# A one-core encoder layer in split fp32: a new order around the norms, the attention fills and the last norm

## The chip, the cores and the metric

The kernel runs on one core of a Trainium2 chip, in one launch. The metric is the device time of one execution in microseconds, as the median of several executions. The core has engines that run side by side, each through a fixed list of instructions: TensorE (PE, matrix products), VectorE (DVE), ScalarE (ACT) and GpSimd (POOL). SyncE (SP) issues most of the DMA transfers; a few are issued from ACT's list. An instruction that waits for a semaphore holds up all that stands behind it on its engine.

## The reference, cut to what matters

x is 512 x 1024 in float32, the inner width of each feed-forward part (FFN) is 2816. The attention projects the normed x to eight heads of differential attention (group A: two score maps for each head, with a relative bias) and eight query heads on two key/value heads (group B: normed and rotated q and k). Every matrix product is wanted at nearly float32 accuracy.

```
def rms_norm(x, g):
    xf = x.astype(jnp.float32)
    y = xf * lax.rsqrt(jnp.mean(xf * xf, axis=-1, keepdims=True) + EPS)
    return (y * g.astype(jnp.float32)).astype(x.dtype)
...
x = x + 0.5 * swiglu(rms_norm(x, ffn1_norm[l]), ffn1_w_gate[l], ffn1_w_up[l], ffn1_w_down[l])
h = rms_norm(x, mix_norm[l])
proj = h @ w_in[l]
...
x = x + jnp.concatenate([oa, ob], axis=-1) @ w_out[l]
x = x + 0.5 * swiglu(rms_norm(x, ffn2_norm[l]), ffn2_w_gate[l], ffn2_w_up[l], ffn2_w_down[l])
return rms_norm(x, final_norm)
```

## The kernel before

**Products.** Every float32 operand is split into two fp32r parts, hi and lo: ACT casts hi (L101), DVE subtracts to get lo (L102), both in `Blocks.parts`. `mm3` (L217) then makes one product of three matmuls. Weights come in blocks: `Blocks.load` (L93, from SP) brings a raw block, two raw buffers deep, and `convert` splits it; `get` hands a block over and, unless `further=False`, splits the next one and loads one more ahead.

**FFN.** x lives in four tiles xn[0..3] of 128 x 1024. The FFN's gate and up products run by a Strassen-like scheme on quarters A11, A12, A21, A22 of the normed, transposed x and on sums S1 to S4 of them (`one_block`); each quarter and sum has hi and lo. The first of the eleven blocks (`first_blocks`) is computed plainly so that it can start while the sums are made. `down` (adds at L484) finishes the tiles in the order t = 2, 3, 0, 1, each in two column halves.

**Norms.** `root` squares a tile on ACT (L292) with a row sum, adds and scales on DVE (L271, L273), and POOL raises to the power -1/2 (L274). `half_T` multiplies (z, L301) and PE transposes z into PSUM (xt, L304). There the gain is per partition, a column `gcol` (L260, an element-wise load, three of them on SP), so `gained` evicts 128 x 256 pieces with ACT (hi, L311) and DVE (lo, L312). `left_first` does tiles 0 and 1 (A11, A12), `left_second` tiles 2 and 3 (A21, A22, S1: L341, L342), `left_sums` the other sums with their splits (L351 to L354). `mix_half` is the same for the attention's input xm.

**Attention.** 64 units (32 of A, then 32 of B; one head and 128 queries each) are written out by hand in a loop, and PE takes that order. Unit i's scores (L743 to L758, L820 to L823), the join of its weights (L768 to L776, L828), the transpose of its weights three units later, its product with v four or five later, and between them fill work by an amount of `FILLS` for each group of units: the remaining projections in `FILL_ORDER`, then the first part of the output projection. The A heads need q and k stacked by DMA (`stack`, L625, 12 issues for each s and head, four for each tile pair); the B heads need k transposed (`make_k2`, PE hT_k, after the 16th step of qb0) and q transposed and copied by DMA (`B_heads`, hT_q and L808, three units ahead). The A output of a pair is normed (o, L794 to L798) and transposed (ot, `finish_O`) seven units behind (`LAG_O`).

**After it.** `out_proj(1)` needs the last B pair (otB); its tiles po_4 to po_7 are added to xn at L916, and after the second of them `half_done` starts FFN2's `left_first`. After the last `down`, `finish` norms each tile for the output: squares, DVE xg = xn * G (L1034), DVE low half (L1038), ACT high half (L1040), issues at L1041.

The order of all engines outside the hand-written loop is set by a planner that goes by priorities and a model of durations; `issue_after` forbids it to place something ahead of a given instruction, `keep_in_program_order` fixes it.

Of the kernel before, what the change touches and what calls it, by code (L numbers as in the profile page):

```python
# [11 lines left out]
F32 = mybir.dt.float32  # L12
# [17 lines left out]
FILL_ORDER = ("qk1", "qk2", "va1", "qk3", "kv", "qb0", "qb1")  # L30
# [4 lines left out]
FILLS = (3.0, 3.0, 3.0, 2.6, 1.3, 1.1, 1.1, 1.1, 2.0)  # L35
LAG_T = 3
LAG_V = {"A": 4, "B": 5}
LAG_O = 7
# [34 lines left out]
class Blocks:  # L73
# [49 lines left out]
    def gate_up(self, t, shape, name):  # L123
# [12 lines left out]
        self.parts(hi[:, 0:4, :], lo[:, 0:4, :], t[:, 0:4, :])  # L136
        for p, n in ((7, 3), (6, 2), (4, 4)):
# [18 lines left out]
def build(ctx, tc, a, out):  # L156
# [92 lines left out]
    def gain_rows(src):  # L249
        g = fpool.tile([P, D], F32, tag="ut", name="G", bufs=1)  # L250
        nc.sync.dma_start(out=g, in_=src.partition_broadcast(P))
# [5 lines left out]
    gcol = {}  # L257
    for nm in ("ffn1", "mix", "ffn2"):
        gcol[nm] = const.tile([P, NK], F32, name=f"gcol_{nm}")
        nc.sync.dma_start(out=gcol[nm], in_=a[f"{nm}_norm"][0].rearrange("(k p) -> p k", p=P))  # L260
        if nm == "ffn1":
            for t in (2, 3):
                nc.sync.dma_start(out=xn[t], in_=xv[:, t, :])
            blocks.load(2)
# [30 lines left out]
    def half_T(half, tags, tag, between=None, parts=2):  # L295

        ps = [bank(tags[kp], f"xt_{tag}{half}{kp}") for kp in range(4)]
        for i in range(2):
            t = 2 * half + i
            r, z = root(t, tag, parts)  # L300
            nc.vector.tensor_scalar_mul(z, xn[t], r)  # L301
            for k in range(NK):
                c = 256 * (k % 2) + P * i
# [14 lines left out]
    def left_first(g, tag, between=None, parts=2):  # L318

        ps = half_T(0, "DDBB", tag, between, parts)  # L320
# [4 lines left out]
        for k in range(NK):  # L325
            gained(L["A11" if k < 4 else "A12"], k % 4, ps[k], g[:, k:k + 1])
        for k in range(NK):
            nc.scalar.activation(raw["A11" if k < 4 else "A12"][:, k % 4, :], ps[k], AF.Copy, scale=g[:, k:k + 1])
        return L, raw

    def left_second(L, raw, g, tag, parts):

        ps = half_T(1, "BCDD", tag, None, parts)
# [42 lines left out]
    def first_blocks(i, L, raw, Hj, g1, second):  # L376
# [23 lines left out]
        for m in "gu":  # L400
            products(m, 1)
# [657 lines left out]
```

## Time and profile before

| | |
|---|---|
| median of 3 executions | 1015.74 us (1014.93 to 1016.44) |
| the profiled execution | 1015.6 us, of which the span is 1013.8 us |
| mean granted TensorE clock | 0.988 |
| busy PE / DVE / ACT / POOL | 974.1 / 720.6 / 489.0 / 227.9 us |
| FFN1 | 0 to 366 us |
| mix norm, first projections | 366 to 407 us |
| attention, A units and B units | 407 to 545 and 545 to 632 us |
| rest of the output projection, FFN2 | 632 to 1003.7 us |
| last norm and output behind the last matmul | 1003.7 to 1013.8 us |

The span runs from the first to the last recorded instruction of the core; the execution's own time has 1.8 us around it. A row of the timeline gives start, duration, engine, line, operation, output<-inputs, and in brackets how long the engine sat idle before it and which instruction ended that wait.

### The profile page before, as it was taken

What the parts mean: (1) busy time and instruction counts of PE and PEld (TensorE: products, weight loads), DVE (VectorE), ACT (ScalarE), POOL (GpSimd) and SP (SyncE); (2) the same over time, 40 slices, a digit from 0 to 9 for tenths busy, and PEclk for the clock granted to TensorE, in tenths of its full rate; (3) what the DMA queues carried; (4) which work ended last, traced back from release to release, by engine and by line L of the source; (5) the groups of instructions that cost most, each with busy time, mean ns of one, the idle gap of its engine ahead of it and who ended that gap; (6) DMA issues with size and microseconds to landing.
All of it is one profiled execution on the core that took longest, in us unless ns stands there. A gap on an engine that the chain in (4) does not pass through costs nothing.

```text
span 1013.8 us, 16666 instructions
## 1 busy us (share of the span) xinstructions
PE 974.1 (96%) x6540; PEld 893.7 (88%) x6540; DVE 720.6 (71%) x1156; ACT 489.0 (48%) x845; POOL 227.9 (22%) x222
## 2 busy tenths in 40 slices
PE   7999999999999999999899989899999999999995
PEld 7999999999888888799888777699999999988884
DVE  5998899988232173777988886689999887842224
ACT  7555444445231162776766665574444454622213
POOL 1232223220000000122656442033222323000001
PEclk8999999999999999999999999999999999999998
DMA  8145534323223325545412121114433423233212
GB/s 244 52 127 188 179 108 126 116 93 109 99 83 106 102 79 144 139 116 158 136 54 58 27 63 52 43 42 125 126 103 106 126 83 125 84 111 118 83 42 83
DMA packets 82399, 105.45 MB, mean 104 GB/s; under 512 B 7873, under 2 KB 66753, under 8 KB 82321
## 3 DMA queue, kind: packets, MB, share of 16 engines
q1 hardware_dynamic: 81744, 103.35, 33.1%
q8 instruction: 51, 0.84, 0.4%
q10 hardware_dynamic: 576, 1.05, 0.3%
q14 instruction: 28, 0.22, 0.1%
HBM read 93.86 MB, written 6.32 MB: 99 GB/s over the span
## 4 chain that ended last, share of the span: by engine, by line
PE 83%; DVE 6%; issue 3%; ACT 2%; DMA 2%; POOL 2%; SPq 1%; POOLq 0%; DVEq 0%; ACTq 0%
PE dn L217 23%; PE bg L217 6%; PE cu L217 6%; PE dg L217 6%; PE du L217 6%; PE bu L217 6%; PE cg L217 6%; PE po L217 3%; PE pqk L217 3%; PE au L217 3%; PE ag L217 3%; PE pva L217 2%; PE poA L217 2%; PE poB L217 1%; PE g L217 1%
## 5 line engine op out<-in xcount | busy, mean ns | idle before, releaser
L102 DVE TENSOR_TENSOR lo_d<-raw_d,hi_d 128x1024 fp32r<-128x1024 f32 x44 | 52.2, 1219 | 84.9 <-ACT hi_d L101 84.9
L132 POOL TENSOR_TENSOR T_g<-raw_g 128x512 f32<-128x512 f32 x40 | 69.1, 1727 | 156.8 <-DVE tl_u L102 75.7
L101 ACT CAST hi_d<-raw_d 128x1024 fp32r<-128x1024 f32 x44 | 44.1, 1051 | 89.8 <-PE dn L217 87.3
L132 POOL TENSOR_TENSOR T_u<-raw_u 128x512 f32<-128x512 f32 x40 | 55.0, 1374 | 128.4 <-DVE tl_g L102 88.9
L101 ACT CAST th_u<-T_u 128x512 fp32r<-128x512 f32 x60 | 37.2, 620 | 88.8 <-PE bg L217 44.6
L101 ACT CAST th_g<-T_g 128x512 fp32r<-128x512 f32 x60 | 37.0, 620 | 46.6 <-PE cu L217 26.5
L758 ACT ACTIVATE s_A<-s_A,m_A 128x512 f32<-128x512 f32 x64 | 45.9, 721 | 25.3 <-DVE m_A L756 25.2
L102 DVE TENSOR_TENSOR lo_g<-raw_g,hi_g 128x1024 fp32r<-128x1024 f32 x44 | 55.7, 1272 | 1.0 <-ACT hi_g L101 0.9
L101 ACT CAST hi_g<-raw_g 128x1024 fp32r<-128x1024 f32 x44 | 44.7, 1047 | 23.6 <-PE dg L217 11.4
L102 DVE TENSOR_TENSOR tl_u<-T_u,th_u 128x512 fp32r<-128x512 f32 x60 | 54.7, 912 | 0.0
L102 DVE TENSOR_TENSOR lo_u<-raw_u,hi_u 128x1024 fp32r<-128x1024 f32 x44 | 53.2, 1216 | 1.6 <-ACT hi_u L101 1.4
L102 DVE TENSOR_TENSOR tl_g<-T_g,th_g 128x512 fp32r<-128x512 f32 x60 | 52.6, 879 | 0.0
L101 ACT CAST hi_u<-raw_u 128x1024 fp32r<-128x1024 f32 x44 | 44.3, 1052 | 15.0 <-PE du L217 12.1
L756 DVE CUSTOM_DVE_ANT_0 s_A<-sA,T 128x512 f32<-128x512 f32 x64 | 42.0, 684 | 9.5 <-PE sA L217 7.5
L829 POOL TENSOR_TENSOR p_B<-p_B,m_B 128x512 f32<-128x512 f32 x32 | 34.5, 1083 | 38.3 <-DVE m_B L828 30.9
L217 PE MATMUL pqk<-xm,hi_qk 128*128 128x512 f32 x128 | 40.3, 396 | 0.0
L217 PEld LDWEIGHTS poA<-va,PT_A 128*128 128x128 f32 x256 | 32.4, 195 | 3.7 <-ACT PT_A L720 3.1
L274 POOL TENSOR_TENSOR r_fin<-r_fin,mhalf 128x1 f32<-128x1 f32 x4 | 2.5, 638 | 145.4 <-DVE r_fin L273 145.4
L217 PE MATMUL poA<-va,PT_A 128*128 128x64 f32 x256 | 33.0, 273 | 2.2 <-ACT PT_A L720 2.2
L274 POOL TENSOR_TENSOR r_mx<-r_mx,mhalf 128x1 f32<-128x1 f32 x4 | 2.2, 552 | 145.0 <-DVE r_mx L273 145.0
L439 ACT ACTIVATE g<-g 128x1024 f32<-128x1024 f32 x20 | 21.2, 1061 | 18.3 <-DVE g L437 18.2
L217 PE MATMUL pqb<-hi_qb,xm 128*128 128x256 f32 x128 | 29.3, 298 | 0.0
(667 smaller groups left out, 3765.3 us busy)
## 6 DMA issues: line engine op xcount, KB each, us to landing
raw_d<-ffn_w_down SPq DMA_DIRECT2D x22, 1024.0 KB, 4.9
raw_g<-ffn_w_gate SPq DMA_DIRECT2D x21, 1024.0 KB, 5.5
raw_u<-ffn_w_up SPq DMA_DIRECT2D x21, 1024.0 KB, 5.4
toep<-nbd SPq DMA_DIRECT2D x8, 512.0 KB, 8.5
raw_qk<-w_in SPq DMA_DIRECT2D x8, 512.0 KB, 4.7
raw_o<-w_out SPq DMA_DIRECT2D x4, 1024.0 KB, 5.5
T<-toep SPq DMA_DIRECT2D x8, 448.0 KB, 4.1
xn<-x SPq DMA_DIRECT2D x4, 512.0 KB, 4.6
```

Of the source, the lines that this page charges most:

```text
L101: self.nc.scalar.copy(out=hi, in_=src)
L102: self.nc.vector.tensor_sub(lo, src, hi.bitcast(F32))
L132: eng.tensor_sub(b12 if n == 1 else T[n], x, T[2] if n == 4 else y)
L217: i = nc.tensor.matmul(*args, **kw)
L274: last["pool"] = nc.gpsimd.tensor_tensor(out=r, in0=r, in1=mhalf[:, 0:1], op=ALU.pow).ins
L439: nc.scalar.activation(g1, g1, AF.Silu)
L756: nc.vector.tensor_tensor_reduce(out=sc, in0=ps, in1=T[:, 384 - P * qt:896 - P * qt], scale=1.0, scalar=BIG, op0=ALU.add, op1=ALU.min, acc ...
L758: nc.scalar.activation(sc, sc, AF.Exp, bias=m[:, s:s + 1], scale=-1.0, accum_out=l1[:, qt, h:h + 1] if s == 0 else l2)
L829: nc.gpsimd.tensor_mul(u["P"], u["P"], l.to_broadcast([P, S]))
```

## The change

- **FFN1's norm.** One gain column is left, loaded from ACT's list ahead of everything; the two others are gone. The transposes of tiles 2 and 3 are held behind the evictions of tiles 0 and 1, the first weight split behind z, and the splits of the sums S behind the main weight split.
- **Mix norm and FFN2's norm.** The gain is loaded as rows (G, 128 x 1024, 512 KB) and multiplied into z by one two-input DVE instruction before the transposes; eviction then takes plain pieces of 128 x 512 (L324, L331), half as many.
- **Attention.** kv's projection is moved ahead of va1 and qk3, make_k2 to the 8th step of qb0, FILLS are given for each four units, the A outputs are transposed nine units behind instead of seven, the B heads are made five units ahead instead of three (three for the first).
- **FFN2's start.** The last block of w_out is got without splitting further; `half_done` runs one tile later; FFN2's first weight split follows z.
- **Last norm.** A fixed order: squares by ACT, low half by DVE straight from xn (L1113), high half of tiles 0 and 1 by DVE and ACT, of tiles 2 and 3 by ACT and a POOL multiplication by G (L1122).

```diff
-FILL_ORDER = ("qk1", "qk2", "va1", "qk3", "kv", "qb0", "qb1")
+FILL_ORDER = ("qk1", "qk2", "kv", "va1", "qk3", "qb0", "qb1")
-FILLS = (3.0, 3.0, 3.0, 2.6, 1.3, 1.1, 1.1, 1.1, 2.0)
+FILLS = (3.0, 3.0, 3.0, 3.0, 3.0, 3.0, 3.0, 2.2, 1.0) + 7 * (1.2,) + (1.4, 1.4)
-LAG_O = 7
+LAG_O = 9
+LEAD_B = (3, 5, 5, 5, 5, 5, 5, 5)
...
-    def gain_rows(src):
...
+    def rows_of(pool, nm, **kw):
+
+        g = pool.tile([P, D], F32, name=f"G_{nm}", **kw)
+        nc.sync.dma_start(out=g, in_=a[f"{nm}_norm"][0].partition_broadcast(P))
         return g
 
+    gcol = const.tile([P, NK], F32, name="gcol")
+    nc.scalar.dma_start(out=gcol, in_=a["ffn1_norm"][0].rearrange("(k p) -> p k", p=P))
     nc.sync.dma_start(out=xn[0], in_=xv[:, 0, :])
...
-            nc.vector.tensor_scalar_mul(z, xn[t], r)
+            if G is None:
+                i = nc.vector.tensor_scalar_mul(z, xn[t], r)
+            else:
+                i = nc.vector.scalar_tensor_tensor(out=z, in0=xn[t], scalar=r, in1=G, op0=ALU.mult, op1=ALU.mult)
+            last["z"] = i.ins
...
+    def evict(hi, lo, p, kp, G):
+
+        for e, col in pieces(kp, G):
+            last["act"] = plain_copy(hi[:, e, :], p[:, e, :], col).ins
+            if col is None:
+                last["dve"] = nc.vector.tensor_sub(lo[:, e, :], p[:, e, :], hi[:, e, :].bitcast(F32)).ins
...
-        ps = half_T(1, "BCDD", tag, None, parts)
+        with tc.issue_after(last["act"]):
+            ps = half_T(1, "BCDD", tag, G, None, parts)
...
-        w["g"] = blocks.get(at["g", i, 0], further=False)
+        with tc.issue_after(last["z"]):
+            w["g"] = blocks.get(at["g", i, 0], further=False)
...
+        with tc.issue_after(blocks.main):
+            left_splits(L, raw, f"f{i + 1}")
...
-            whi, wlo = blocks.get(at[("o", part, hh)])
+            whi, wlo = blocks.get(at[("o", part, hh)], further=(part, hh) != (1, 1))
+            if (part, hh) == (1, 1):
+                blocks.load(at["u", 1, 0] + 1)
...
-                if part == 1 and hh == 1 and t0 == 1:
+                if part == 1 and hh == 1 and t0 == 2:
                     st["half_done"]()
...
-                if nm == "qb0" and w == 15:
+                if nm == "qb0" and w == 8:
                     make_k2()
...
+    def fin_steps(t, h, add):
+        prev = {3: 2, 0: 3, 1: 0}.get(t)
+        if (t, h) == (1, 0):
+            root_of(0)
+        fixed(add())
+        if h == 0 and prev in (2, 3):
+            mean_of(prev)
+            root_of(prev)
+        square(t, h)
+        if h == 0 and prev is not None:
+            high_half(prev)
+        if h == 1 and prev in (2, 3):
+            low_half(prev)
+        if (t, h) == (0, 1):
+            mean_of(0)
+            weighted(0)
+        if (t, h) == (1, 1):
+            mean_of(1)
+            weighted(1)
+            root_of(1)
+            low_half(0)
+            low_half(1)
+            high_half(1)
+
+    down(1, H, steps=fin_steps)
```

The planner's order at three places. First ACT at the start of FFN1 (z_f squares tiles xn_95 to xn_98, which are x's tiles 0 to 3; A11f1h is an eviction). Before:

```order
L292 ACTIVATE z_f_121,ss_f_122<-xn_95 128x1024
L292 ACTIVATE z_f_139,ss_f_140<-xn_96 128x1024
L101 CAST hi_g_193<-raw_g_101 128x1024 x2
L292 ACTIVATE z_f_259,ss_f_260<-xn_97 128x1024
L311 ACTIVATE A11f1h<-xt_f_117,gcol_ffn_104 128x256
L311 ACTIVATE A11f1h<-xt_f_118,gcol_ffn_104 128x256
L292 ACTIVATE z_f_274,ss_f_275<-xn_98 128x1024
L311 ACTIVATE A12f1h<-xt_f_119,gcol_ffn_104 128x256
```

After:

```order
L102 CAST hi_g_189<-raw_g_103 128x1024 x2
L324 ACTIVATE A11f1h<-xt_f_113,gcol 128x256
L324 ACTIVATE A11f1h<-xt_f_114,gcol 128x256
L324 ACTIVATE A12f1h<-xt_f_115,gcol 128x256
L324 ACTIVATE A12f1h<-xt_f_116,gcol 128x256
L324 ACTIVATE A11f1h<-xt_f_113,gcol 128x256
L324 ACTIVATE A11f1h<-xt_f_114,gcol 128x256
L324 ACTIVATE A12f1h<-xt_f_115,gcol 128x256
L324 ACTIVATE A12f1h<-xt_f_116,gcol 128x256
L292 ACTIVATE z_f_255,ss_f_256<-xn_97 128x1024
L292 ACTIVATE z_f_270,ss_f_271<-xn_98 128x1024
```

The squares of tiles 2 and 3 moved behind all eight evictions of hi.

Second PE in the A units, where the keys of group B are transposed (hT_k, from kn) between score products (sA) and the fill qb0 (pqb). Before:

```order
L217 MATMUL pqb_5249<-lo_qb_4917,xm_3698 128x256
L217 MATMUL pqb_5249<-hi_qb_4916,xm_3698 128x256
L217 MATMUL sA_00_5376<-st_kqk_4888,st_qqk_4884 128x512
L217 MATMUL sA_01_5381<-st_kqk_4896,st_qqk_4892 128x512
L222 MATMUL hT_k_5393<-ident,kn_5223 64x128
L222 MATMUL hT_k_5393<-ident,kn_5239 64x128
L222 MATMUL hT_k_5393<-ident,kn_5054 64x128
L222 MATMUL hT_k_5393<-ident,kn_5070 64x128
```

After:

```order
L219 MATMUL pqb_5231<-hi_qb_4941,xm0l 128x256
L219 MATMUL poA_5154<-va,PT_A_2_5250 128x64 x4
L224 MATMUL pt_A_3_5290<-ident,pm_A_3_5142 128x128 x4
L224 MATMUL hT_k_5298<-ident,kn_4660 64x128
L224 MATMUL hT_k_5298<-ident,kn_4676 64x128
L224 MATMUL hT_k_5298<-ident,kn_4512 64x128
L224 MATMUL hT_k_5298<-ident,kn_4528 64x128
```

hT_k stood behind the scores of unit 24, with kn's last two tiles produced shortly ahead of it; it now stands two units earlier, behind the scores of unit 22, and kv, from which kn comes, is projected two fills earlier.

Third DVE where FFN2 starts (xn<-po adds the output projection's tiles, lo_g is FFN2's first weight split). Before:

```order
L916 TENSOR_TENSOR xn_97<-po_2_6830,xn_97 128x512
L916 TENSOR_TENSOR xn_98<-po_3_6847,xn_98 128x512
L102 TENSOR_TENSOR lo_g_6894<-raw_g_6761,hi_g_6893 128x1024 x2
L916 TENSOR_TENSOR xn_95<-po_4_6901,xn_95 128x512
L271 TENSOR_TENSOR r_f_6937<-ss_f_6934 128x1
L916 TENSOR_TENSOR xn_96<-po_5_6915,xn_96 128x512
L273 TENSOR_SCALAR r_f_6937<-r_f_6937 128x1
L301 TENSOR_SCALAR z_f_6933<-xn_95,r_f_6937 128x1024
```

After:

```order
L966 TENSOR_TENSOR xn_98<-po_3_6846,xn_98 128x512
L966 TENSOR_TENSOR xn_97<-po_6_6907,xn_97 128x512
L966 TENSOR_TENSOR xn_95<-po_4_6879,xn_95 128x512
L271 TENSOR_TENSOR r_f_6929<-ss_f_6926 128x1
L273 TENSOR_SCALAR r_f_6929<-r_f_6929 128x1
L305 SCALAR_TENSOR_TENSOR z_f_6925<-xn_95,r_f_6929,G_ffn_6548 128x1024
L966 TENSOR_TENSOR xn_96<-po_5_6893,xn_96 128x512
L271 TENSOR_TENSOR r_f_6946<-ss_f_6943 128x1
L273 TENSOR_SCALAR r_f_6946<-r_f_6946 128x1
L305 SCALAR_TENSOR_TENSOR z_f_6942<-xn_96,r_f_6946,G_ffn_6548 128x1024
L103 TENSOR_TENSOR lo_g_6998<-raw_g_6738,hi_g_6997 128x1024 x2
L966 TENSOR_TENSOR xn_98<-po_7_6977,xn_98 128x512
```

lo_g moved from ahead of tile 0's last add to behind the second z.

On SP the twelve loads of a head's stacks for the third pair after the first (st_qqk and st_kqk from qk30, qk31) now have the load of the second block of w_out between them, which waits for the raw buffer that qb1's split frees; and the T tables of heads 6 and 7 stand ahead of them.

## Rows read from the trace of the kernel before

**Rows 1.** The page: span, and PE's busy time, share and instructions.

```profile
span 1013.8 us, 16666 instructions
...
PE 974.1 (96%) x6540; PEld 893.7 (88%) x6540; DVE 720.6 (71%) x1156; ACT 489.0 (48%) x845; POOL 227.9 (22%) x222
```

**Rows 2.** Stretches: start:end, length, busy time of PE, PEld, DVE, ACT, POOL, clock, DMA.

```profile
13.00:19.40 6.40, 6.34 (x26) 5.73 (x27) 5.54 (x15) 6.40 (x15) 0.97 (x2) 0.50 0.64 128
...
500.00:550.00 50.00, 43.91 (x332) 41.10 (x333) 42.66 (x114) 33.48 (x80) 27.36 (x39) 0.97 0.21 53
```

**Rows 3.** Waits of PE, whole span: what waited, for what: total us, times, longest.

```profile
PE hT_k L222 <- DVE kn L685: 3.6, 2, 3.2
...
PE g L217 <- ACT A11f1h L311: 3.2, 1, 3.2
...
PE ot L222 <- DVE o L798: 2.5, 1, 2.5
...
PE sB L217 <- DMA qh<-qh: 2.4, 2, 1.9
...
PE bg L217 <- DVE lo_g L102: 2.3, 2, 1.9
...
PE po L217 <- ACT otB L101: 1.4, 1, 1.4
```

**Rows 4.** Timeline of the start: ACT and PE.

```profile
8.99 1.05 ACT L101 CAST hi_g<-raw_g 128x1024 fp32r<-128x1024 f32 x1 [0.65 <-DMA raw_g<-ffn_w_gate]
...
11.45 1.06 ACT L292 ACTIVATE z_f<-xn 128x1024 f32<-128x1024 f32 x1 [1.41 <-DMA xn<-x]
...
12.51 0.82 ACT L311 ACTIVATE A11f1h<-xt_f,gcol_ffn 128x256 fp32r<-128x256 f32 x2
...
13.02 0.80 PE L217 MATMUL g<-A11f1h,hi_g 128*128 128x256 f32 x2 [3.17 <-ACT A11f1h L311]
```

**Rows 5.** Timeline, 30 to 52 us: POOL, DVE and PE's first product with S4.

```profile
31.24 2.28 POOL L132 TENSOR_TENSOR T_u<-raw_u 128x512 f32<-128x512 f32 x1
...
32.28 2.32 DVE L351 TENSOR_TENSOR S3rf<-A11rf,A21rf 128x1024 f32<-128x1024 f32 x1
...
35.13 1.21 DVE L351 TENSOR_TENSOR S4rf<-A12rf,S2rf 128x1024 f32<-128x1024 f32 x1
...
46.99 1.21 DVE L354 TENSOR_TENSOR S4f1l<-S4rf,S4f1h 128x1024 fp32r<-128x1024 f32 x1
...
51.62 0.28 PE L217 MATMUL dg<-S4f1l,hi_g 128*128 128x256 f32 x1
```

**Rows 6.** Groups by line and form, 366 to 407 us: the mix norm's evictions by DVE.

```profile
L312 DVE SCALAR_TENSOR_TENSOR xm<-xt_mx,gcol_mix,xm 128x256 fp32r<-128x256 f32 x16 | 6.8, 478 | 1.4 <-ACT xm L311 1.4
```

**Rows 7.** Timeline of SP, 479 to 488 us: the third q/k stacks after the first.

```profile
479.64 1.15 SPq L625 DMA_DIRECT2D st_qqk<-qk30h  x2
...
485.89 1.22 SPq L625 DMA_DIRECT2D st_kqk<-qk31h  x2
```

**Rows 8.** Timeline where FFN2 starts: DVE, then PE.

```profile
639.84 2.35 DVE L102 TENSOR_TENSOR lo_g<-raw_g,hi_g 128x1024 fp32r<-128x1024 f32 x2
...
642.11 0.68 DVE L916 TENSOR_TENSOR xn<-po,xn 128x512 f32<-128x512 f32 x1
...
645.39 0.75 DVE L301 TENSOR_SCALAR z_f<-xn,r_f 128x1024 f32<-128x1024 f32 x1 [0.67 <-POOL r_f L274]
...
646.29 1.06 PE L304 MATMUL xt_f<-ident,z_f 128*128 128x128 f32 x8 [2.35 <-DVE r_f L271]
```

**Rows 9.** Timeline of the end: PE's last matmul, ACT and its queue.

```profile
1003.28 0.39 PE L217 MATMUL dn<-hi_d,h110l 128*128 128x512 f32 x1
...
1006.52 0.72 ACT L1040 ACTIVATE z_fin<-xg_fin,r_fin 128x512 f32<-128x512 f32 x1 [2.18 <-POOL r_fin L274]
...
1007.15 0.61 ACT L292 ACTIVATE z_fin<-xn 128x512 f32<-128x512 f32 x1
...
1010.26 0.34 ACTq L1041 DMA_DIRECT2D out<-z_fin  x1
```

More of the change, by code (lines that the diff above doesn't have):

```diff
@@ L256, in build @@
     blocks.load(1)
[L257 to L264, printed above, removed]
+    for t in (2, 3):
+        nc.sync.dma_start(out=xn[t], in_=xv[:, t, :])
+    blocks.load(2)
     def rsqrt(ss, tag):
@@ L293, in root, with half_T @@
         return rsqrt(ss[:, :parts], f"{tag}{t}"), z
-    def half_T(half, tags, tag, between=None, parts=2):
+    def half_T(half, tags, tag, G=None, between=None, parts=2):
         ps = [bank(tags[kp], f"xt_{tag}{half}{kp}") for kp in range(4)]
@@ L483, in down, with add @@
                 cs = slice(512 * h, 512 * h + 512)
-                nc.vector.tensor_add(xn[t][:, cs], acc[t, h], xn[t][:, cs])
-            done(t)
+                def add(t=t, h=h, cs=cs):
+                    return nc.vector.tensor_add(xn[t][:, cs], acc[t, h], xn[t][:, cs])
+                if steps:
+                    steps(t, h, add)
+                else:
+                    add()
+            if done:
+                done(t)
     def temp(shape, name):
@@ L1027, in build @@
     ov = out.rearrange("(t p) c -> p t c", p=P)
-    def finish(t):
-        r, y = root(t, "fin")
-        xg_ = fpool.tile([P, D], F32, tag="H", name=f"xg_fin{t}", bufs=NJ)
-        for h in range(2):
-            c = slice(512 * h, 512 * h + 512)
-            nc.vector.tensor_mul(xg_[:, c], xn[t][:, c], G[:, c])
-        for h in range(2):
-            c = slice(512 * h, 512 * h + 512)
-            if h == 0:
-                nc.vector.tensor_scalar_mul(y[:, c], xg_[:, c], r)
-            else:
-                nc.scalar.activation(y[:, c], xg_[:, c], AF.Copy, scale=r)
-            (nc.sync if h == 0 else nc.scalar).dma_start(out=ov[:, t, c], in_=y[:, c])
@@ L1043, in build, with fixed, square @@
-    down(1, H, finish)
+    r_, y_, xg_, ss_ = {}, {}, {}, {}
+    half = (slice(0, 512), slice(512, D))
+    def fixed(i):
+        tc.keep_in_program_order(i)
+    def square(t, h):
+        if h == 0:
+            y_[t] = fpool.tile([P, D], F32, tag="H", name=f"y_fin{t}", bufs=NJ)
+            xg_[t] = fpool.tile([P, 512], F32, tag="H", name=f"xg_fin{t}", bufs=NJ)
+            ss_[t] = const.tile([P, 2], F32, tag="ss", name=f"ss_fin{t}", bufs=4)
+            r_[t] = const.tile([P, 1], F32, tag="r", name=f"r_fin{t}", bufs=4)
+        fixed(nc.scalar.activation(y_[t][:, half[h]], xn[t][:, half[h]], AF.Square, accum_out=ss_[t][:, h:h + 1]))
@@ new lines, in mean_of, with root_of, weighted @@
+    def mean_of(t):
+        fixed(nc.vector.tensor_scalar(out=r_[t], in0=ss_[t][:, 0:1], scalar1=1.0 / D, scalar2=EPS,
+                                      op0=ALU.mult, op1=ALU.add))
+    def root_of(t):
+        fixed(nc.vector.scalar_tensor_tensor(out=r_[t], in0=ss_[t][:, 1:2], scalar=1.0 / D, in1=r_[t],
+                                             op0=ALU.mult, op1=ALU.add))
+        fixed(nc.gpsimd.tensor_tensor(out=r_[t], in0=r_[t], in1=mhalf[:, 0:1], op=ALU.pow))
+    def weighted(t):
+        fixed(nc.vector.tensor_mul(xg_[t], xn[t][:, half[1]], G[:, half[1]]))
@@ new lines, in write, with low_half, high_half @@
+    def write(t, h, eng):
+        eng.dma_start(out=ov[:, t, half[h]], in_=y_[t][:, half[h]])
+    def low_half(t):
+        fixed(nc.vector.scalar_tensor_tensor(out=y_[t][:, half[0]], in0=xn[t][:, half[0]], scalar=r_[t],
+                                             in1=G[:, half[0]], op0=ALU.mult, op1=ALU.mult))
+        write(t, 0, nc.sync)
+    def high_half(t):
+        if t in (0, 1):
+            fixed(nc.scalar.activation(y_[t][:, half[1]], xg_[t], AF.Copy, scale=r_[t]))
+        else:
+            fixed(nc.scalar.activation(xg_[t], xn[t][:, half[1]], AF.Copy, scale=r_[t]))
+            fixed(nc.gpsimd.tensor_mul(y_[t][:, half[1]], xg_[t], G[:, half[1]]))
+        write(t, 1, nc.scalar if t == 1 else nc.sync)
```

111 lines of the change are left out of this document (66 added, 45 removed).

## The prediction

> **What bounds the kernel now.** I read the page first: PE is busy 974.1 of the 1013.8 us span [rows 1], so PE sets the time and, since the change leaves PE's matmuls as they are, all that it can win lies in the 39.7 us in which PE stands still, in PE's slow stretches, and in the tail behind its last matmul. Then I read the waits of PE, which name the places: the keys' transposes hT_k wait 3.2 us at once for kn, the first gate product g 3.2 us for A11, ot 2.5 us for o, a B score 1.9 us for the copied query qh, a gate product 1.9 us for lo_g, the output projection 1.4 us for otB [rows 3]. The stretches show what else is full there: from 500 to 550 us PE is busy 43.91 us, and DVE 42.66 us of the 50 [rows 2]. Last I read the timeline at each place that the change touches. All sums are made against the profiled execution, 1015.6 us (span 1013.8 plus 1.8 around it); the median of the runs, 1015.74, is 0.14 us above it. About 0.2%, 2.0 us, is what a measurement of this kernel can tell from no change.
>
> **FFN1's start: 3.4 us less.** The first eviction A11f1h starts at 12.51 on ACT, behind the square of tile 2, which had waited 1.41 us for its tile to land; PE's first product follows at 13.02, after 3.17 us idle [rows 4]. In the new order that square and the next stand behind all eight evictions, so the first eviction follows the cast of hi_g, which ends at 8.99 + 1.05 = 10.04 [rows 4], if the gain column has landed by then; it is now issued first, from ACT. An eviction reaches PE 0.51 us after its start (12.51 to 13.02), so PE starts at about 10.5 and 2.5 us are won. After the idle stretch the granted clock is 0.50 from 13.0 to 19.4, that is 1.2 GHz, with PE busy 6.34 us [rows 2]; the same work at 2.4 GHz is half, so up to 3.2 us more could come if the shorter pause spares the clock: 5.7 us as the upper end. What limits it is DVE: S4's split ends at 46.99 + 1.21 = 48.20, and PE's first recorded product that reads it begins at 51.62 [rows 5]. PE is thus 3.4 us behind DVE. On DVE's list the split of S4 stands five rows further back, behind a whole weight split that used to come after it; against that, the evictions ahead come earlier. I take it that it stays at about 48.2, and PE can then come forward by 3.4 us and no more. The lower end is 1: DVE's evictions, which follow two halves of lo_g, hold PE for most of the gap.
>
> **Mix norm: 0.3 us less.** 16 evictions of 128x256 by DVE at 478 ns (7.6 us) [rows 6] become 8 of 128x512 at 0.68 us, the price of an add of that size out of PSUM [rows 8] (5.4 us). Half of the 2.2 us falls on the second half, the one on the path, of which the last piece counts: 1.1 us. Against it z becomes a two-input instruction of 128x1024, 1.21 us as S4rf [rows 5] in place of 0.75 us [rows 8], 0.45 us more; and the first piece, twice as large, comes 0.2 us later. 1.1 - 0.45 - 0.2 is about 0.4; I take 0.3, between -1 (the gain tile not yet there, or the large piece setting the pace) and 2. The 512 KB of G go out from SP long before, in the products of FFN1.
>
> **Attention: 6.5 us less.** Four waits lose their cause: hT_k (3.2) gets kn from a projection made two fills earlier, ot (2.5) comes nine units behind instead of seven, the queries are made five units ahead (1.9), and with fill work left over the last projection has other matmuls ahead of those that need otB (1.4): 9.0 us [rows 3]. One comes new: the third pair's ot, two units later, stands directly ahead of the output projection's matmuls that read it. These wait for one eviction by ACT and one by DVE, 0.68 us each by the PSUM add [rows 8]: 1.2 us, which leaves 7.8. Next in line is DVE. If the 500 to 550 stretch lost all of PE's 6.1 idle us, it would hold 42.66 us of DVE in 43.9, 97% [rows 2]. I therefore take 1.3 us back. The bounds: 2 if what is removed in the A units all turns into waits for DVE, and of the B units' 5.8 less the new 1.2 under half remains; 10 if even the small waits beside them shrink.
>
> **FFN2's start: 1.2 us less.** DVE's lo_g takes 2.35 us at 639.84, and only at 642.11 follows the add of tile 0; PE then idles 2.35 us until the first transposes [rows 8]. With lo_g behind the second z that add can come when its matmuls are done, about 1.2 us sooner by half of lo_g's length, and z costs 0.45 more: 0.75 won. lo_g now lies between the second z and the first gate product, 2.35 us, and only one output tile's twelve matmuls cover it; their price is that of a 128x512 matmul every 0.23 us, 2.8 us, so it just fits. Halving the evictions ahead of the sums wins some of the 1.9 us that a gate product waited for the next lo_g [rows 3]; I take 0.45 of it. The range is -2 (lo_g uncovered) to 2.5.
>
> **Last norm: 2.0 us less.** The last matmul starts at 1003.28 and the last issue at 1010.26. Between them the last tile's squares wait on ACT behind an older tile's high half (1006.52, which waited 2.18 us for POOL), and begin at 1007.15 [rows 9]. In the fixed order, by durations of the rows: the add of the last half ends about 1004.5 (1003.28 + 0.39 + 0.18 + 0.68), its square about 1005.4, mean and root 1006.2, two low halves of 0.68 on DVE and one high half of 0.72 on ACT about 1007.2. That is 3.0 us sooner. A collision can take 1.1 of it: DVE's two-input S3rf of 128x1024 took 2.32 us beside POOL's 2.28 us instruction, S4rf of the same size 1.21 alone [rows 5], and the new POOL multiplications run beside DVE's two-input ones. So 2.0, between 0.3 and 3.0. The Trainium skill, page SBUF — State Buffer, section SBUF: two separate sides, speaks against this part: a two-input DVE instruction and a GpSimd one share a port pair under an exclusive lock, and the loser stands still for the whole of the other. Here the trace agrees, with 1.1 us lost; by the rule alone both multiplications would stop DVE, and this part would give 3.0 - 2.2 = 0.8.
>
> **Sum.** 3.4 + 0.3 + 6.5 + 1.2 + 2.0 = 13.4; 1015.6 - 13.4 = 1002.2 us.
>
> **Rivals.**
> - DVE becomes the bound of the A units. For it: 42.66 of 50 us busy; against it: the projections' evictions move earlier, to stretches with less fill behind them. Attention then gives 3.0: 1002.2 + 3.5 = 1005.7. Chance 0.22.
> - The start stays. The clock falls as before, and S4's split, now behind a weight split (2.35 us [rows 8]), comes later: the start gives 1.0, 1004.6. For it: DVE's longer list; against: its evictions start sooner. Chance 0.13.
> - DVE is stopped twice in the last norm, by both POOL multiplications, at 1.1 us each [rows 5]: the part gives 0.8 of its 3.0, 1003.4. Chance 0.10.
> - SP holds the third pair's stacks, and the kernel gets slower. The twelve copies of a head took from 479.64 to 487.11, 7.5 us [rows 7]. All but three of them now stand behind a load that waits for qb1's weight split on DVE. It decides if that split ends later than about 1 us before the two A units (4.3 us each, 138 us for 32) that stand ahead of the first score to read them: 8.6 less 7.5. If heads 6 and 7 each lost a whole 7.5, 15.0 would outweigh 13.4: 1017.2. Against it: the split stands in DVE's order behind unit 21's scores, in time by a little. Chance 0.08.
> - The gains show, but each is nearly used up at its own place (low ends together, 0.3 in sum): 1015.3. Chance 0.05.
>
> **How the numbers follow.** My forecast has the remaining 0.42, and the first three rivals, 0.45, are faster as well: faster 0.87, same 0.05, slower 0.08. All high ends together would be 23.2 us, 992.4; all low ends 1015.3. They are not met together: 994 to 1010 leaves out the last two rivals (0.13) and a few per cent below, and holds the rest.
>
> **What would show it.** Right: PE's first g at about 10.5; no wait of hT_k for kn and of ot for o above 1 us; PE's first transposes of FFN2 after less than 2 us idle; the last issue some 5 us or less behind the last matmul's start. Wrong: PE waits in the A units under other names (scores for m_A, poA for PT_A) that sum to over 5 us; a wait of a score for the stacks of qk3; S4's split after 49 us; DVE instructions in the tail of twice their length. If the sum of PE's waits falls by less than 6 us, the forecast has failed.

## The result and the profile after

The changed kernel takes 1002.75 us in the median of three executions (1002.03 to 1003.99) against 1015.39 before, 12.6 us less, where 13.4 were forecast; the ratio is 0.9872 (95% interval 0.9859 to 0.9885). A fourth execution of it took 3824.40 us, for a reason that no run shows, and is left out. In two later measurements, on two chips, the same kernel stood at 0.9860 (0.9845 to 0.9875) and 0.9870 (0.9854 to 0.9886) of the kernel before. The mean of the three, 0.9867, is the measure for the experiments below; 0.001 is 1.0 us, and with intervals of 0.0015 on either side a difference of two such ratios is known to about 2 us. Where the changed kernel was measured on the same chip beside an experiment, the difference from that measurement is given as well.

The page of the changed kernel answers to [rows 1]:

```profile
span 1002.2 us, 16621 instructions
...
PE 972.4 (97%) x6540; PEld 893.4 (89%) x6540; DVE 727.0 (73%) x1132; ACT 482.2 (48%) x823; POOL 239.2 (24%) x224
```

The span is 11.6 us shorter: PE's idle time went from 39.7 to 29.8 us, and its busy time is 1.7 us less. The waits of PE, over the whole span, answer to [rows 3]:

```profile
PE poA L219 <- ACT PT_A L768: 2.1, 3, 1.4
PE sA L219 <- DVE m_A L804: 2.1, 2, 1.6
PE sB L219 <- ACT p_B L871: 1.9, 2, 1.2
PE g L219 <- DVE A11f2l L331: 1.8, 1, 1.8
PE po L219 <- ACT ot L778: 1.7, 1, 1.7
...
PE g L219 <- DVE A11f1l L333: 1.3, 2, 0.8
PE xt_f L309 <- DVE z_f L305: 1.2, 1, 1.2
PE xt_f L309 <- DVE z_f L303: 1.1, 1, 1.1
...
PE ag L219 <- DVE lo_g L103: 1.0, 1, 1.0
```

The waits of hT_k, of ot, of a score for qh and of po for otB are gone, and so is that of bg for lo_g in FFN2 (1.9 us); new ones are po for ot (1.7), g for A11's low part in FFN2 (1.8) and in FFN1 (1.3). The stretches answer to [rows 2], the columns are the same:

```profile
13.00:19.40 6.40, 5.84 (x35) 5.64 (x36) 5.74 (x15) 6.40 (x15) 1.68 (x3) 0.73 0.82 251
500.00:550.00 50.00, 46.12 (x354) 42.55 (x353) 46.46 (x115) 35.02 (x81) 31.55 (x42) 1.00 0.28 82
```

From 500 to 550 us PE is busy 46.12 us in place of 43.91, and DVE 46.46 in place of 42.66: there DVE is now as full as PE. From 13.0 to 19.4 us the granted clock is 0.73 in place of 0.50.

Where the time came from, by starts of PE's matmuls in the two profiles, in us:

| place | before | after | gained there | forecast |
|---|---|---|---|---|
| first down product of FFN1 | 246.50 | 243.84 | 2.7 | 3.4 |
| first score of the A units | 407.12 | 404.72 | -0.3 | 0.3 |
| last product of the B units with v | 632.63 | 623.70 | 6.5 | 6.5 |
| first down product of FFN2 | 883.80 | 873.50 | 1.4 | 1.2 |
| last matmul to the end of the span | 10.54 | 9.23 | 1.3 | 2.0 |

The two later profiles of the changed kernel give at the same five places gains of 2.3, 1.2, 8.4, 1.4, 1.2 us (after_again) and 3.1, 1.2, 6.6, 2.1, 1.2 us (after_third): what one profile shows for a place is known to 1 to 2 us.

### The profile page after: what moved, and what is told of

It reads as the page before. It is cut to its first block, busy times and chain, and to the rows that moved or that the text cites. A ratio compares the mean times of both kernels' runs of the same rounds, so it can differ in the third digit from the quotient of the medians.

```text
span 1002.2 us, 16621 instructions
## 1 busy us (share of the span) xinstructions
PE 972.4 (97%) x6540; PEld 893.4 (89%) x6540; DVE 727.0 (73%) x1132; ACT 482.2 (48%) x823; POOL 239.2 (24%) x224
## 4 chain that ended last, share of the span: by engine, by line
PE 84%; DVE 7%; DMA 3%; issue 2%; ACT 2%; POOL 2%; SPq 1%; POOLq 0%; DVEq 0%; ACTq 0%
PE dn L219 24%; PE bg L219 5%; PE cg L219 5%; PE cu L219 5%; PE bu L219 5%; PE dg L219 5%; PE du L219 5%; PE po L219 3%; PE pqk L219 3%; PE ag L219 3%; PE au L219 3%; PE g L219 3%; PE u L219 2%; PE pva L219 1%; DMA gb_k<-k_norm 1%
## 5 line engine op out<-in xcount | busy, mean ns | idle before, releaser
L133 POOL TENSOR_TENSOR T_g<-raw_g 128x512 f32<-128x512 f32 x40 | 77.9, 1947 | 146.8 <-DVE tl_u L103 75.4
L102 ACT CAST th_g<-T_g 128x512 fp32r<-128x512 f32 x60 | 36.7, 619 | 41.4 <-PE cu L219 21.2
L219 PE MATMUL po<-hi_o,ot 128*128 128x512 f32 x64 | 27.3, 426 | 1.8 <-ACT ot L778 1.7
L871 ACT ACTIVATE p_B<-sB,m_B 128x512 f32<-128x512 f32 x32 | 22.1, 691 | 12.2 <-DVE m_B L868 9.8
```

The source lines that it names most:

```text
L133: eng.tensor_sub(b12 if n == 1 else T[n], x, T[2] if n == 4 else y)
L219: i = nc.tensor.matmul(*args, **kw)
L871: nc.scalar.activation(pm, ps, AF.Exp, bias=m[:, 0:1], scale=1.0, accum_out=m[:, 1:2])
```

## The experiments

Each kernel is the changed one with the edit shown; several parts were undone one at a time, so that a part is worth what its kernel is slower.

**FFN1's start undone (u1_start).**

```diff
-    nc.scalar.dma_start(out=gcol, in_=a["ffn1_norm"][0].rearrange("(k p) -> p k", p=P))
     nc.sync.dma_start(out=xn[0], in_=xv[:, 0, :])
     nc.sync.dma_start(out=xn[1], in_=xv[:, 1, :])
     blocks.load(1)
+    nc.sync.dma_start(out=gcol, in_=a["ffn1_norm"][0].rearrange("(k p) -> p k", p=P))
...
-        with tc.issue_after(last["act"]):
+        with ExitStack() as held:
+            if tag != "f1":
+                held.enter_context(tc.issue_after(last["act"]))
             ps = half_T(1, "BCDD", tag, G, None, parts)
```

(and the same for the two other holds, of the weight split and of the sums' splits).

> The changed kernel with FFN1's start put back: the gain column issued from SP behind the first weight block, tiles 2 and 3, the first weight split and the sums' splits no longer held behind anything. Theory (each place has its own gain, and they add): FFN1's down products began 2.7 us sooner in the changed kernel's profile, so this kernel is 2.7 us slower than it, about 1006.0 us, with PE's first g product near 13.0 again. Rival (the start is set by DVE's list, PE's earlier start is lost before the sums are split): under 1 us slower, about 1003.9.

Measured: 1004.37 us, ratio 0.9894 (0.9881 to 0.9908), that is 2.7 us slower than the changed kernel; PE's first g product at 12.80, FFN1's down from 247.03, where the three profiles of the changed kernel have 243.37 to 244.20. The theory's number holds, and the rival (under 1 us) falls by the place.

**The attention's schedule undone (u2_attn).** All four settings and the place of make_k2 as before (FILLS written out for each four units).

```diff
-FILL_ORDER = ("qk1", "qk2", "kv", "va1", "qk3", "qb0", "qb1")
+FILL_ORDER = ("qk1", "qk2", "va1", "qk3", "kv", "qb0", "qb1")
-FILLS = (3.0, 3.0, 3.0, 3.0, 3.0, 3.0, 3.0, 2.2, 1.0) + 7 * (1.2,) + (1.4, 1.4)
+FILLS = 6 * (3.0,) + 2 * (2.6,) + 2 * (1.3,) + 6 * (1.1,) + 2 * (2.0,)
-LAG_O = 9
-LEAD_B = (3, 5, 5, 5, 5, 5, 5, 5)
+LAG_O = 7
+LEAD_B = 8 * (3,)
...
-                if nm == "qb0" and w == 8:
+                if nm == "qb0" and w == 15:
```

> The changed kernel with the old attention schedule: old order of the fills and old amounts, keys transposed after the 16th step of qb0, A outputs seven units behind, B heads three units ahead. Theory (the four removed waits, 9 us, less 1.2 us new and 1.3 us given to DVE): 6.5 us slower than the changed kernel, about 1009.9, with hT_k, ot, the score for qh and po for otB waiting again, about 9 us together. Rival (DVE bounds the A units, the waits only changed their names): 3 us slower, about 1006.4.

Measured: 1007.38 us, 0.9931 (0.9914 to 0.9948), 6.5 us slower. The waits of PE in this kernel show the old ones back:

```profile
PE hT_k L224 <- DVE kn L733: 3.7, 2, 3.2
PE ot L224 <- DVE o L846: 2.5, 1, 2.5
...
PE sB L219 <- DMA qh<-qh: 1.4, 1, 1.4
```

That is 7.6 us of waits; otB's did not return. From the last product with v to FFN2's first transposes this kernel takes 13.4 us, the changed one 14.7: the new fill amounts leave 1.3 us more of the output projection behind the units. So of the time that the table shows in the units, 1.3 us is only moved.

**Its three settings one at a time (u2a_order, u2b_lag, u2c_lead).** u2a_order has the first two and the last line pairs of the diff above, u2b_lag only `LAG_O = 7`, u2c_lead only `LEAD_B = 8 * (3,)`.

> The changed kernel with the old order and amounts of the fills and the keys transposed after the 16th step of qb0; A outputs still nine units behind, B heads five units ahead. Theory (each wait has its own part of the change): hT_k waits 3.2 us again and po for otB 1.4, 4.6 us slower than the changed kernel. Rival (the A units are bound by DVE, what the keys gain is lost there): 1.5 us slower or less.

> The changed kernel with the A outputs seven units behind again. Theory: ot waits 2.5 us for o again and the wait of po for ot (1.4 to 1.9) stays or shrinks, 1 to 2.5 us slower than the changed kernel. Rival (the later transposes only traded one wait for the other): no difference.

> The changed kernel with every B head made three units ahead again. Theory: one score waits about 2 us for the copied query, 2 us slower. Rival (the wait had its cause in the order of the fills): no difference.

Measured: 1003.19 us, 0.9881 (0.9866 to 0.9895), 1.4 us slower; 1004.97 us, 0.9900 (0.9884 to 0.9916), 3.3 us slower; 1005.50 us, 0.9904 (0.9889 to 0.9920), 3.8 us slower. Against the changed kernel measured beside each it is 2.4, 3.0 and 3.5 us. Their waits of PE:

```profile
PE hT_k L224 <- DVE kn L733: 3.7, 2, 3.2
```

```profile
PE ot L224 <- DVE m_B L876: 3.8, 1, 3.8
PE sA L219 <- DVE m_A L804: 2.9, 3, 1.6
...
PE hT_k L224 <- ACT PT_A L768: 1.1, 1, 1.1
```

```profile
PE poA L219 <- ACT PT_A L768: 3.0, 3, 1.7
PE sB L219 <- DMA qh<-qh: 2.1, 1, 2.1
...
PE po L219 <- ACT ot L778: 1.0, 1, 1.0
```

In u2a_order hT_k waits its 3.7 us in full, yet the kernel loses only 1.4 to 2.4: its A units, first score to first B score, take 131.0 us against 128.1 to 129.7 in three profiles of the changed kernel, and its B units, from there to the last product with v, 88.7 against 89.0 to 90.7. The theory's 4.6 falls, and the loss lies near the rival's 1.5: PE's other waits in the A units sum to 3.4 us here and to 5.0 to 5.2 in the changed kernel, so about half of what the keys' earlier transposes take off goes into them. That DVE is the bound there is not shown by this: of the 1.6 to 1.8 us that came, 0.6 are waits for DVE (hT_q for qn), 0.2 to 0.6 for ACT (poA for PT_A) and 0.4 to 0.7 for the stacks' DMA. The two other settings show in the B units (93.0 and 93.3 us), and by the medians each alone costs somewhat more than its wait did; in u2b_lag ot stands behind other work of DVE and waits 3.8 us, not 2.5. The single losses sum to 8.5, the joint one is 6.5. That the settings no longer fit each other when one is undone is a likely reading of it, but a difference of 2 us between such sums is within what is known.

**FFN2's start undone in order (u3_ffn2).**

```diff
-            whi, wlo = blocks.get(at[("o", part, hh)], further=(part, hh) != (1, 1))
-            if (part, hh) == (1, 1):
-                blocks.load(at["u", 1, 0] + 1)
+            whi, wlo = blocks.get(at[("o", part, hh)], further=True)
...
-                if part == 1 and hh == 1 and t0 == 2:
+                if part == 1 and hh == 1 and t0 == 1:
...
-        with tc.issue_after(last["z"]):
+        with ExitStack() as held:
+            if not i:
+                held.enter_context(tc.issue_after(last["z"]))
```

> The changed kernel with FFN2's start put back in order alone (first weight split ahead of z, norm begun one output tile earlier, one more block split and loaded ahead), the gain rows kept. Theory: the order gives 1.2 us, so 1004.6 us, with a wait of over 2 us before the first transposes. Rival (what FFN2's start won comes from the gain rows' larger and fewer evictions, and the order only moves the wait from the transposes to the first product): no difference within 0.5 us, 1003.4.

Measured: 1001.18 us, 0.9860 (0.9845 to 0.9875): 0.7 us faster than the changed kernel, which is no difference. The waits of PE from 620 to 700 us, first of this kernel, then of the changed one (after_third):

```profile
PE xt_f L309 <- DVE r_f L271: 2.9, 1, 2.9
PE cg L219 <- DVE S1f2l L103: 0.7, 1, 0.7
PE ag L219 <- DVE lo_g L103: 0.3, 1, 0.3
PE bg L219 <- DVE lo_g L103: 0.2, 1, 0.2
```

```profile
PE g L219 <- DVE A11f2l L331: 1.8, 1, 1.8
PE xt_f L309 <- DVE z_f L305: 1.8, 2, 1.2
```

By the medians the rival holds: no loss shows, and the wait moves from the transposes to the first product. In place it does not. The waits sum to 4.1 us here and to 3.0 to 3.6 in the changed kernel's three profiles, and the stretch from the last product with v to FFN2's first down product takes 251.6 us, against 249.1 to 249.8 in those three and at most 250.6 in five other kernels that leave this place alone (u1_start, u2a_order, u2c_lead, u4_tail, v2). v1 below, which also puts lo_g ahead of the second z, takes 251.6 as well. So the order may be worth the theory's 1.2 us; medians that are known to 2 us can't tell, and it stays open.

**The last norm undone (u4_tail).** `finish` as before in place of the fixed order.

> The changed kernel with the old last norm. Theory: the end lies 10.5 us behind the start of the last matmul again in place of 9.2, 1.3 us slower, about 1004.7. Rival (the end is set by the output transfers themselves, whose issue order alone changed): within 0.5 us, 1003.4.

Measured: 1002.20 us, 0.9872 (0.9859 to 0.9886), 0.5 us slower, within what is known; in the profile the span ends 10.50 us behind the start of the last matmul, in the changed kernel's three profiles 9.23 to 9.33. The 1.2 us are there in place, as the theory had them.

**Gain columns in place of rows (u5_cols),** loaded into the same buffers at the same places.

```diff
-        g = pool.tile([P, D], F32, name=f"G_{nm}", **kw)
-        nc.sync.dma_start(out=g, in_=a[f"{nm}_norm"][0].partition_broadcast(P))
+        g = pool.tile([P, NK], F32, name=f"G_{nm}", **kw)
+        nc.sync.dma_start(out=g, in_=a[f"{nm}_norm"][0].rearrange("(k p) -> p k", p=P))
...
+            i = nc.vector.tensor_scalar_mul(z, xn[t], r)
...
+        col = gcol if G is None else G
+        return [(slice(e, e + 1), col[:, 2 * kp + e:2 * kp + e + 1]) for e in range(2)]
```

> The changed kernel with the mix norm's and FFN2's gain as columns again, loaded at the same places as the rows, so that only z, the evictions and the size of the load go back. Theory (the larger, fewer evictions were worth 0.3 us at the mix norm and about as much at FFN2's start): 0.6 us slower than the changed kernel. Rival (the rows carry most of what the order of FFN2's start does not explain): 2 us or more slower, the stretch from the first down product of FFN1 to the first A score 1.2 us longer, as it was before.

Measured: 1002.50 us, 0.9877 (0.9862 to 0.9892), 1.0 us slower, or 1.7 against the changed kernel measured beside it; from the first product of va to the first A score 36.9 us against 36.7 in two profiles of the changed kernel, and from the last product with v to FFN2's first down product 251.0 against 249.1 to 249.8. The rows are worth some tenths at the mix norm, where the rival expected 1.2, and 1 to 2 us in all, most of it in FFN2. In size that lies between the theory's 0.6 and the rival's 2, which the noise does not tell apart.

**The changed kernel again (after_again, after_third).**

> The changed kernel once more, beside the others of this call, as the measure for them: 0.987 of the kernel before by the first runs, about 1002 us here if the kernel before takes about 1015.

> The changed kernel beside the others of this call, as their measure: 0.986 to 0.987 of the kernel before.

Measured: 1000.80 us, 0.9860, and 1001.99 us, 0.9870, as given above. Eight executions of these two spread from 1000.16 to 1002.99 us, and the ends of the spread go with the mean granted clock: 1000.16 and 1000.59 at 0.996, 1002.61 at 0.991, 1002.99 at 0.989 (between them it does not decide: 1000.94 and 1002.65 both stand at 0.992).

**Three places altered (v1).**

```diff
-    nc.scalar.dma_start(out=gcol, in_=a["ffn1_norm"][0].rearrange("(k p) -> p k", p=P))
...
     blocks.load(1)
+    nc.sync.dma_start(out=gcol, in_=a["ffn1_norm"][0].rearrange("(k p) -> p k", p=P))
...
-        with tc.issue_after(last["z"]):
+        with tc.issue_after(last["po" if i else "z"]):
...
-        if t in (0, 1):
+        if t in (0, 1, 3):
...
+        if (t, h) == (3, 1):
+            weighted(3)
...
             weighted(1)
+            low_half(0)
             root_of(1)
-            low_half(0)
```

(`last["po"]` is the output projection's add into tile 1.)

> The changed kernel with three places altered. (1) The gain column is issued from SP behind the first weight block: if it was the column's small packets, issued first, that let x's tile 1 land 1.3 us later than before, PE's first g product comes at about 10.5 in place of 11.7 and FFN1's down begins 1 us sooner; if the column itself is then late, the first product comes no sooner. (2) FFN2's first weight split stands behind tile 1's add, ahead of its z: the product that waited 1.8 us for A11's low part waits about 0.5, the transposes of tile 1 come 1.6 us later, under a wait that stays below that: 0.7 us won; rival: the wait only moves, nothing won. (3) In the last norm only tile 2 uses the POOL multiplication, and the low half of tile 0 stands ahead of the last root: no DVE instruction meets a POOL one late in the norm, and the span ends 8.0 us behind the start of the last matmul in place of 9.2; rival (the collision is not on the chain): 9.2 stays. Together 2.9 us less than the changed kernel, or nothing by the rivals.

Measured: 1002.16 us, 0.9872 (0.9856 to 0.9889), 0.5 us slower than the changed kernel (1.4 against the one measured beside it), no gain. Each part can be read from its place. (1) The start of the changed kernel, then of v1:

```profile
0.74 0.46 ACTq L258 DMA_DIRECT2D gcol<-ffn_norm  x1
...
7.25 1.06 ACT L292 ACTIVATE z_f<-xn 128x1024 f32<-128x1024 f32 x1 [1.52 <-DMA xn<-x]
...
11.20 0.83 ACT L324 ACTIVATE A11f1h<-xt_f,gcol 128x256 fp32r<-128x256 f32 x2
...
11.72 0.51 PE L219 MATMUL g<-A11f1h,hi_g 128*128 128x256 f32 x2 [0.57 <-ACT A11f1h L324]
```

```profile
5.69 1.06 ACT L292 ACTIVATE z_f<-xn 128x1024 f32<-128x1024 f32 x1 [0.19 <-DMA xn<-x]
...
9.96 0.83 ACT L324 ACTIVATE A11f1h<-xt_f,gcol 128x256 fp32r<-128x256 f32 x2
...
10.48 0.50 PE L219 MATMUL g<-A11f1h,hi_g 128*128 128x256 f32 x2 [0.73 <-ACT A11f1h L324]
```

The column's packets, issued first, delayed x's tile 1: its square starts at 7.25, and 1.56 us sooner with the column behind the weights (u1_start, which moves the column too, has it at 5.78); g starts at 10.48, 1.24 us sooner, and the column is not late. With the shorter pauses the clock stays up, in the stretch from 12 to 20 us first of the changed kernel's first profile, then of a later one (after_third), then of v1:

```profile
12.00:20.00 8.00, 6.67 (x42) 6.25 (x42) 7.34 (x17) 7.78 (x19) 2.28 (x3) 0.79 0.79 246
```

```profile
12.00:20.00 8.00, 7.51 (x39) 7.01 (x39) 7.34 (x17) 7.78 (x19) 2.29 (x3) 0.59 0.79 246
```

```profile
12.00:20.00 8.00, 7.44 (x63) 7.24 (x63) 5.68 (x15) 8.00 (x18) 2.80 (x3) 1.00 0.74 233
```

The first u product comes at 19.88 in place of 22.83 (after_third). Of these 3 us little is left when FFN1's down begins, 243.28 against 243.37 to 244.20: a product of a later block waited 1.5 us for its weight split (ag for lo_g), a wait that is 1.0 in the changed kernel's first profile and 0.4 in v2's. (2) FFN2's first g product comes 2.0 us later, counted from the last product with v: the rival, and worse. (3) The span still ends 9.2 us behind the last matmul's start: the DVE product that took the place of tile 3's POOL multiplication met the one that was left, tile 2's, as the timeline of v1 shows:

```profile
986.85 1.39 POOL L1124 TENSOR_TENSOR y_fin<-xg_fin,G 128x512 f32<-128x512 f32 x1 [0.84 <-ACT xg_fin L1123]
...
987.00 1.78 DVE L1109 TENSOR_TENSOR xg_fin<-xn,G 128x512 f32<-128x512 f32 x1
```

**Another three (v2).** The column as in v1; FFN2 as in the changed kernel; the A outputs' transposes ahead of the products with v; no POOL multiplication in the last norm.

```diff
         fill(rate / 2)
+        u = at_lag(i, LAG_O)
+        if u and u["kind"] == "A" and last_of_pair(u):
+            O_T(u)
         for kind, lag in LAG_V.items():
...
-        u = at_lag(i, LAG_O)
-        if u and u["kind"] == "A" and last_of_pair(u):
-            O_T(u)
...
+        if (t, h) in ((2, 1), (3, 1)):
+            weighted(t)
...
-            fixed(nc.scalar.activation(xg_[t], xn[t][:, half[1]], AF.Copy, scale=r_[t]))
-            fixed(nc.gpsimd.tensor_mul(y_[t][:, half[1]], xg_[t], G[:, half[1]]))
```

(`high_half` is the first branch for all tiles; `low_half(0)` stands ahead of `root_of(1)`.)

> The changed kernel with three places altered. (1) The gain column from SP behind the first weight block: PE's first g product at 10.5, as measured with this edit, and FFN1's down products 0.9 us sooner. (2) The A outputs' transposes ahead of the unit's product with v and weight transposes: the third pair's eviction is covered, the 1.4 to 1.9 us wait of po for ot goes, the B units end 1.5 us sooner; rival: o is not normed by then, and ot waits instead. (3) No POOL multiplication in the last norm, every high half by DVE and ACT, the low half of tile 0 ahead of the last root: if POOL's collision with DVE is what holds the end, the span ends about 8.3 us behind the start of the last matmul in place of 9.3; rival (DVE's own load holds it): 9.3 stays. Together 3.4 us less than the changed kernel, or 0.9 by the rivals.

Measured: 995.79 us against 1001.99 of the changed kernel measured beside it, 0.9811 (0.9794 to 0.9827) of the kernel before: 6.2 us faster than the changed kernel, the fastest of all. FFN1's down products begin at 241.82 against 243.37; first B score to last product with v takes 86.3 us against 89.2, with no wait of po for ot left; the span ends 8.1 us behind the last matmul's start against 9.3. The rivals fall at all three places, and the gain is larger than the 3.4 forecast: 1.5 us at the start (0.9 forecast), 2.8 in the B units (1.5) and 1.2 at the end (1.0), with 0.7 in the A units that nothing forecast; the two profiles' mean granted clocks are 0.998 and 0.992. The end of the changed kernel, then of v2:

```profile
991.95 1.29 POOL L1122 TENSOR_TENSOR y_fin<-xg_fin,G 128x512 f32<-128x512 f32 x1 [0.84 <-ACT xg_fin L1121]
992.01 1.78 DVE L1107 TENSOR_TENSOR xg_fin<-xn,G 128x512 f32<-128x512 f32 x1
...
996.71 0.98 POOL L1104 TENSOR_TENSOR r_fin<-r_fin,mhalf 128x1 f32<-128x1 f32 x1 [2.24 <-DVE r_fin L1102]
...
998.48 0.39 ACTq L1110 DMA_DIRECT2D out<-y_fin  x1
```

```profile
984.34 0.68 DVE L1107 TENSOR_TENSOR xg_fin<-xn,G 128x512 f32<-128x512 f32 x1
...
988.08 0.54 POOL L1104 TENSOR_TENSOR r_fin<-r_fin,mhalf 128x1 f32<-128x1 f32 x1 [2.33 <-DVE r_fin L1102]
...
989.41 0.40 ACTq L1110 DMA_DIRECT2D out<-y_fin  x1
```

In the changed kernel DVE's product with G takes 1.78 us beside POOL's multiplication and the last POOL root 0.98 beside a two-input DVE instruction; in v2 they take 0.68 and 0.54, and the last issue on ACT's queue comes 4.3 us behind the start of the last matmul (985.07) in place of 5.5 (992.98).

## Why the prediction was right, step by step

The forecast time, 1002.2, lies 0.6 us below the median, and the sum of 13.4 us compares with 12.6 in the first measurement, 14.2 and 13.0 in the later ones. That PE's waits were the thing to win from holds: its idle time fell by 9.9 us. That the total came so near is in part luck. In the first profile the start, the mix norm and the last norm fell short by 0.6 to 0.7 us each and the attention by 1.3, net of what it only moved, while FFN2's start gave 1.5 more than forecast. Of the four signs of being right, two came (no wait of hT_k or ot above 1 us; FFN2's first transposes after 1.24 us idle) and two did not (g at 11.72 and not 10.5; the last issue 5.5 us behind the last matmul's start and not 5). Of the four signs of being wrong, three came, each with a small price: a score waited for qk3's stacks, S4's split ended after 49 us, and a DVE instruction of the tail took more than twice its length. By steps:

- **Start, 3.4 forecast, 2.7 found, in place (2.3 to 3.1 in the three profiles) and by undoing it.** Two statements in it were wrong. g was to start at 10.5 and started at 11.72, since the column that was issued first held up x's tile 1; I had counted the column's landing, not what it pushes aside. The Trainium skill, page DMA: Bandwidth & Descriptors, section Issuing engines are not separate DMA queues, says that transfers issued from several engines run on the same 16 DMA engines and interleave; v1 agrees, with 1.56 us for the tile behind the column. And the limit from S4's split was none: in the changed kernel it ended at 50.09, 1.9 us later than before, and FFN1's down still began 2.7 us sooner. In v2 it begins 4.7 us sooner than before.
- **Mix norm, 0.3 forecast.** u5_cols shows about 0.2. The clock decides more there: from 360 to 380 us it is at 0.91 in the profile of before and in the first of the changed kernel, and at 1.00 in the two later ones, where the stretch from va's first product to the first A score takes 36.7 us in place of 38.0 and 38.2. So the stage shows a loss of 0.3 us in the table, and a gain of 1.2 in each of the two others. One execution of the changed kernel and another (after, then after_third):

```profile
360.00:380.00 20.00, 18.32 (x119) 16.53 (x118) 13.52 (x23) 8.54 (x19) 1.66 (x3) 0.91 0.23 75
```

```profile
360.00:380.00 20.00, 18.32 (x132) 16.48 (x131) 14.39 (x22) 8.97 (x20) 1.65 (x3) 1.00 0.20 65
```

- **Attention, 6.5 forecast, 6.5 found** by undoing it and in place; with 1.3 us of the latter only moved behind the units and three profiles at 6.5, 8.4 and 6.6, the net is 5 to 7. The three corrections were needed: po did wait for ot (1.7, forecast 1.2), DVE did fill up (46.46 of 50 us), and hT_k's 3.2 us were worth about 1.4 to 2.4. Of the rival of a DVE-bound stretch this much is true, that about half of hT_k's wait went into other waits of the A units, and the sum had taken 1.3 us back for it; that DVE is their cause is shown for a third of them.
- **FFN2's start, 1.2 forecast.** What failed is "lo_g just fits": the twelve matmuls covered none of it. They ran from 639.05 to 642.06, while the second z was made, and lo_g began only as they ended; between it and A11's low part stood tile 3's add, and g waited 1.8 us:

```profile
641.67 0.39 PE L219 MATMUL po<-hi_o,otB 128*128 128x512 f32 x1
...
641.91 2.35 DVE L103 TENSOR_TENSOR lo_g<-raw_g,hi_g 128x1024 fp32r<-128x1024 f32 x2
...
645.51 0.58 PE L219 MATMUL g<-A11f2l,hi_g 128*128 128x256 f32 x1 [1.83 <-DVE A11f2l L331]
```

  This place still gained 1.4 us although 1.3 us of work came to it from the units, because bg's wait for the next lo_g went whole (1.9 us [rows 3], of which the sum had 0.45): PE's waits there were 2.4 + 1.9 = 4.3 us before and are 1.2 + 1.8 = 3.0. How that divides between the order and the rows stays open. Undoing either alone (u3_ffn2, u5_cols) brings these waits to 4.1 us and lengthens the stretch by 1.2 to 2.5, but by the medians u3_ffn2 loses nothing and u5_cols about 1.
- **Last norm, 2.0 forecast, 1.3 found.** One collision cost 1.1 us, as counted (1.78 against 0.68); the other POOL multiplication stopped no product of DVE. A second kind had not been counted, POOL's root beside the low half (0.98 against 0.54), though the kernel before has such a root too, of 0.93 us at 1002.42. How much of the missing 0.7 is the root's is not shown: v1, whose last root took 0.54, still ended 9.2 us behind. And the 3.0 were too much by themselves: v2, without either collision, ends 2.4 us sooner than the kernel before. The Trainium skill's rule on the shared port (page SBUF — State Buffer, section SBUF: two separate sides) agrees with these rows: DVE's 992.01 instruction ends 0.55 us behind POOL's, and the POOL root ends 0.4 us behind DVE's, each by somewhat less than its own length (0.68 and 0.54). The 0.8 that was reckoned by the rule lies somewhat nearer to 1.3 than my 2.0, but it counted two stopped products, and one was stopped.
- **The slower rival** did not come: a score waited 0.6 to 0.9 us for the last pair's stacks, once in each profile.

## What to carry to other kernels

A wait's length in the list is not the price of its removal: here 3.7 us of one wait were worth 1.4 to 2.4, since other waits grew, and 2.1 us of another came with a loss of 3.5 to 3.8. So undo each part alone and read its stage, not the total only: the last norm's 1.2 us were clear in place and lost in the spread of the medians. What is issued first competes with the transfers that the start waits for, though it comes from an idle queue and has few bytes: here a column of 4 KB cost 1.56 us. Before work is moved to GpSimd at the end of a program, look for two-input VectorE instructions beside it: here ACT and DVE alone ended 1.2 us sooner.

## What the runs showed that was not expected

The granted clock decided about a microsecond at several places by itself. Behind the same pause of PE ahead of the first product of va (1.0 to 1.1 us in the changed kernel's waits), the stretch from 360 to 380 us ran at 0.91 in one execution and at 1.00 in two others, and the time from that product to the first A score was 38.2 us against 36.7. The B units took 90.7 us at 0.98 in the first of these profiles and 89.0 at 1.00 in the second. At the start the pauses differ with the clock. Ahead of the second transposes the changed kernel's PE pauses 1.10 us in its first profile, 1.68 and 1.81 in the two others (after, then after_third):

```profile
10.06 1.09 PE L309 MATMUL xt_f<-ident,z_f 128*128 128x128 f32 x8 [1.10 <-DVE z_f L303]
```

```profile
10.05 1.09 PE L309 MATMUL xt_f<-ident,z_f 128*128 128x128 f32 x8 [1.81 <-DVE z_f L303]
```

With about 0.57 us more ahead of g in all three, the stretch from 12 to 20 us runs at 0.79 in the first and at 0.59 in the two others; v1 pauses at most 0.78 there and stays at 1.00, that is 2.4 GHz. Against after_third its first u product comes 3 us sooner, 1.2 of them by the earlier first g; the other 1.7 come with the clock.
